# A recurrence in two halves: a state of keys times values instead of the scores between the halves

## The chip, the cores and the metric

The kernel runs on one core of a Trainium2 chip. The metric is device time in microseconds (us) of one execution. TensorE does the matrix products, VectorE, ScalarE and GpSimd the elementwise work, and SyncE issues the transfers of weights and activations.

## What is computed

Two layers of an encoder over 512 positions and 1024 features: a mixer layer with three branches, then cross attention and a feed-forward layer. One of the branches is a gated linear recurrence (HGRN2) with eight heads, in both directions; the change is in it alone. For each head and direction, cut to what matters:

```
f     = lb + (1 - lb) * sigmoid(z)           # decay per position and key feature (128)
log_f = log(max(f, TINY));  key = (1 - lb) * sigmoid(-z)
state = state * f + key^T value              # state is 128 x 64
o     = q . state                            # 64 values per position
o_total = rmsnorm(o_forward + o_backward, g_out) * silu(g)
```

The reference does it in chunks of 16 positions with the state carried over (`_gated_scan`); the backward direction is the same on the flipped sequence.

## The kernel before

It holds no state at all. For every pair of positions it forms a score, the query decayed from a reference point times the key decayed up to it, and then one product of scores with values gives the output of both directions. Per head:

- `take_q`, `take_z` take the projected query and the two gates out of PSUM (ScalarE; two sigmoids per direction).
- `hgrn_decay`, once per direction d: ScalarE's L407, VectorE's two clips L410 and L411, ScalarE's two logarithms L412 and L413, GpSimd's sum L414, the running sum along the sequence on VectorE (`scan`, L417), small sums at 16 reference points, three exponentials on ScalarE (L437, L441, L442), decayed queries `qd` (L444) and inverse-decayed keys `ki` (L445), and eight products L463 into the tile `lt`: four levels i of block sizes (32, 64, 128, 256 positions) for keys (VectorE) and for queries (GpSimd).
- `hgrn_scores`: TensorE's score matmuls. 64 small ones for the diagonal blocks of 128 positions (banks `bd`, `bb`), then the cross scores in three banks `g`, eight matmuls with 1536 columns in all: four of 128 columns within a half of the sequence and four of 256 between the halves. Two masked copies take the diagonal out (L491, L492), ScalarE's L494 and VectorE's four small additions L496 put it into the tile `a`, and three copies L511 on ScalarE put the cross scores there.
- the output block, once per pair of heads: eight matmuls of 512 columns with the values as weights (64 wide, the pair's two heads on opposite halves of the output's partitions).

The heads run as a pipeline: while head i's scores and the projections of head i + 2 are on TensorE, the elementwise engines do the decay of the next head. All other TensorE work in the stretch is projections: each weight arrives from memory as `wraw`, is split into a high part `whi` (ScalarE, L120) and a low part `wlo` (VectorE, L121), and takes three matmuls (L151) per 128 x 128 block, so a projection to 128 columns is 24 matmuls. The order of each engine's instructions is fixed when the kernel is built, by a scheduler that takes TensorE's program order as it is written; every engine runs its own list strictly in that order.

Of the kernel before, what the change touches and what calls it, by code (L numbers as in the profile page):

```python
# [12 lines left out]
AF = mybir.ActivationFunctionType  # L13
ALU = mybir.AluOpType
AX = mybir.AxisListType

P = 128
D = 1024
T = 512
# [56 lines left out]
class _K:  # L76
# [214 lines left out]
    def hgrn(self, l, x, xg, acc, sd):  # L291


        nc = self.nc
        lv = V_N * l
        ar = np.arange(P)
        heads = [dict(n=i) for i in range(8)]
        off = dict(q=O_BQ, f=O_FF, b=O_FB, i=O_BI, g=O_BG)
        proj = lambda o, n: self.projs("w_in", l, np.arange(D), [off[o] + n * P + ar], h)[0]
        vs, st = {}, {}  # L300

        def take_q(hd, b):
            hd["q"] = self.t2()
            nc.scalar.activation(hd["q"], b, AF.Copy)

        def take_z(hd, zs, gs=()):
            for c, b in gs:
                self.gate_put(sd, c, b)
            for d, z in enumerate(zs):
                s, k = self.t2(), self.t2()  # L310
                nc.scalar.activation(s, z, AF.Sigmoid)
                last = nc.scalar.activation(k, z, AF.Sigmoid, scale=-1.0)
                hd[d] = (s, k)
            hd["pin"] = self.pin(last)

        def late():
            st["r"] = self.rstd(acc, 1024)
            st["h"] = self.normed(x, st["r"], lv + V_GMIX)

        def decay(hd):  # L320
            hd["qk"] = self.c8([P, 4, T])
            with self.tc.issue_after(hd["pin"].ins):
                for d in range(2):
                    self.hgrn_decay(l, hd, d)

        def values(n):
            st["vf"] = self.t2()
            nc.scalar.activation(st["vf"], proj("i", n), AF.Copy)

        b0, b1, bq, bv = self.projs("w_in", l, np.arange(D), [off[o] + ar for o in "fbqi"], xg, late, 3)  # L330
        h, r = st["h"], st["r"]
        take_z(heads[0], [self.timed(b, r) for b in (b0, b1)])
        heads[0]["q"] = self.timed(bq, r)
        st["vf"] = self.timed(bv, r)
        decay(heads[0])
        g0, g1, b0, b1 = self.projs("w_in", l, np.arange(D), [O_GB + ar, O_GB + P + ar, off["f"] + P + ar,
                                                             off["b"] + P + ar], h)
        take_z(heads[1], [b0, b1], [(0, g0), (1, g1)])
        take_q(heads[1], proj("q", 1))
        vs[0] = self.vturn(st["vf"])  # L340
        values(1)
        self.hgrn_scores(heads[0])
        decay(heads[1])
        y = self.pairs4(4)
        for i in range(8):
            pr = i // 2
            if i > 0:
                self.hgrn_scores(heads[i])
            if i % 2 == 0:
                if 0 < i < 6:  # L350
                    values(pr + 1)
            gs = [(i + 2, self.gate_proj(l, O_GB, i + 2, h))] if i < 6 else []
            if i % 2 == 1:
                g = proj("g", pr)
                sg = self.t2()
                last = nc.scalar.activation(sg, g, AF.Sigmoid)
                if i == 7:
                    self.pin(last)
                nc.vector.tensor_tensor(sg, g, sg, op=ALU.mult)
            if i < 6:  # L360
                take_z(heads[i + 2], [proj("f", i + 2), proj("b", i + 2)], gs)
            elif i == 6:
                pre = self.mla_pre(l, h)
                for nm in ("ckv0", "ckv1", "key"):
                    pre[nm]()
            else:
                for nm in ("cq0", "nckv", "cq1", "rope"):
                    pre[nm]()
            if i % 2 == 1:

                ob = self.bank()
                for j in range(4):
                    for e in range(2):
                        hf = slice(64 * e, 64 * e + 64)
                        self.mm(ob[hf], vs[pr][:, j, hf], heads[i - 1 + e]["a"][:, j * T:(j + 1) * T], j == 0, j == 3)
                osb, sq = self.t2(), self.t2()
                nc.scalar.activation(osb, ob, AF.Copy)
                nc.scalar.activation(sq, osb, AF.Square)
            if i < 6:
                take_q(heads[i + 2], proj("q", i + 2))  # L380
                if i % 2 == 0:
                    vs[pr + 1] = self.vturn(st["vf"])
            elif i == 7:
                pre["cq2"]()
            if i % 2 == 1:
                ob = self.bank()
                self.mm(ob, self.cst[:, C_BONE:C_BONE + P], sq, True, True)
            if i < 6:
                decay(heads[i + 2])
            elif i == 7:  # L390
                pre["ncq"]()
            if i % 2 == 1:
                r = self.t2()
                self.rsqrt(r, ob, 64)
                nc.vector.scalar_tensor_tensor(r, osb, self.col(lv + V_GOUT), r, op0=ALU.mult, op1=ALU.mult)
                nc.vector.tensor_tensor(r, r, sg, op=ALU.mult)
                self.split(y[pr][0], y[pr][1], r)
        return y, h

    def hgrn_decay(self, l, hd, d):  # L400

        nc = self.nc
        tt = nc.vector.tensor_tensor
        c = d * 8 + hd["n"]
# [4 lines left out]
        g = self.t2()  # L409
# [37 lines left out]
        for i in range(4):  # L447
            n, nb = 1 << i, 8 >> i
            for w, (src, ex) in enumerate(((qd, eq), (ki, ek))):
                half = (1 - d) if w == 0 else d  # L450
                eng = nc.gpsimd if w == 0 else nc.vector
                sv = src.rearrange("p (b s n i) -> p b s n i", s=2, n=n, i=32)[:, :, half]
                ev = ex[:, 16 * i:16 * i + 16].rearrange("p (b s n) -> p b s n", s=2, n=n)[:, :, half]
                ov = lt[:, i, w].rearrange("p (b n i) -> p b n i", n=n, i=32)
                if n == 1:
                    sv, ev, ov = sv[:, :, 0], ev[:, :, 0], ov[:, :, 0]
                    ev = ev.unsqueeze(2).to_broadcast([P, nb, 32])
                elif nb == 1:
                    sv, ev, ov = sv[:, 0], ev[:, 0], ov[:, 0]
                    ev = ev.unsqueeze(2).to_broadcast([P, n, 32])  # L460
                else:
                    ev = ev.unsqueeze(3).to_broadcast([P, nb, n, 32])
                eng.tensor_tensor(ov, sv, ev, op=ALU.mult)  # L463
        hd["lt", d] = lt

    def hgrn_scores(self, hd):

        nc = self.nc
# [6 lines left out]
        for j in range(4):  # L475
# [9 lines left out]
            for g in range(4):  # L485
# [1 line left out]
                lt = lf if g < 2 else lr  # L487
                cs = slice(64, 128) if g < 2 else slice(0, 64)
                one(bd[q4[g], j, cs], lt[:, 1, 1, ks], lt[:, 1, 0, 64 * j:64 * j + 64])
        a = self.c8([P, 4 * T])  # L490
        nc.vector.copy_predicated(self.zz, self.msk[:, 0].unsqueeze(1).to_broadcast([P, 4, P]), bd)  # L491
        nc.vector.copy_predicated(self.zb, self.msk[:, 1, 0:32].unsqueeze(1).to_broadcast([P, 4, 32]), bb)  # L492
        dg = bass.AP(a.tensor, a.offset, [list(a.ap[0]), [640, 4], [1, P]])
        nc.scalar.activation(dg, self.zz, AF.Copy)  # L494
        for g in range(4):
            tt(dg[q4[g], :, q4[g]], self.zz[q4[g], :, q4[g]], self.zb[q4[g]], op=ALU.add)  # L496
        h0, h1 = slice(0, P), slice(P, 2 * P)
        for i in range(3):
            g = self.bank()
            if i == 0:  # L500
                one(g[:, 0:128], lf[:, 2, 1, h0], lf[:, 2, 0, h0])
                one(g[:, 128:384], lf[:, 3, 1, h0], lf[:, 3, 0])
                one(g[:, 384:512], lr[:, 2, 1, h0], lr[:, 2, 0, h0])
            elif i == 1:
                one(g[:, 0:256], lf[:, 3, 1, h1], lf[:, 3, 0])
                one(g[:, 256:512], lr[:, 3, 1, h0], lr[:, 3, 0])
            else:
                one(g[:, 0:128], lf[:, 2, 1, h1], lf[:, 2, 0, h1])
                one(g[:, 128:384], lr[:, 3, 1, h1], lr[:, 3, 0])
                one(g[:, 384:512], lr[:, 2, 1, h1], lr[:, 2, 0, h1])  # L510
            nc.scalar.activation(a[:, i * 640 + 128:(i + 1) * 640], g, AF.Copy)  # L511
        hd["a"] = a

    def gates(self, l, gate, h):

# [17 lines left out]
    def gate_put(self, sd, c, b):  # L533
        sg = self.t2()
        last = self.nc.scalar.activation(sg, b, AF.Sigmoid)
        self.nc.sync.dma_start(sd[:, c], sg)
        return last

    def branch(self, l, sd, wname, rows, y, merged, first):

# [639 lines left out]
```

## Time and profile before

| | |
|---|---|
| median of 3 runs | 2372.4 us (2371.82 to 2373.35) |
| the profiled execution | 2371.25 us, its span 2369.5 us |
| busy share | TensorE 99%, VectorE 62%, ScalarE 50%, GpSimd 7% |
| granted TensorE clock, mean | 0.999 of full speed |

The rows are one execution, seen instruction by instruction. A row of a timeline gives start, length, engine, line, operation, output and inputs, and in brackets the idle time before it with what ended it. The length of a row reaches a little into the next one's, so costs are better taken from start to start.

### The profile page before, as it was taken

What the parts mean: (1) busy time and instruction counts of PE and PEld (TensorE: products, weight loads), DVE (VectorE), ACT (ScalarE), POOL (GpSimd) and SP (SyncE); (2) the same over time, 40 slices, a digit from 0 to 9 for tenths busy, and PEclk for the clock granted to TensorE, in tenths of its full rate; (3) what the DMA queues carried; (4) which work ended last, traced back from release to release, by engine and by line L of the source; (5) the groups of instructions that cost most, each with busy time, mean ns of one, the idle gap of its engine ahead of it and who ended that gap; (6) DMA issues with size and microseconds to landing.
All of it is one profiled execution on the core that took longest, in us unless ns stands there. A gap on an engine that the chain in (4) does not pass through costs nothing.

```text
span 2369.5 us, 34666 instructions
## 1 busy us (share of the span) xinstructions
PE 2336.9 (99%) x12934; PEld 1901.6 (80%) x12934; DVE 1469.8 (62%) x2753; ACT 1187.3 (50%) x2162; POOL 167.8 (7%) x165
## 2 busy tenths in 40 slices
PE   9999999999999999999999999999999999999998
PEld 7877778777888888888887777777788888888886
DVE  8876756566756555355577866666657575553553
ACT  7766566556545433233367656655555454332332
POOL 1332300000000000000013322000000000000000
PEclk9999999999999999999999999999999999999999
DMA  4223233234553233333432223322345523333332
GB/s 163 86 86 94 84 96 103 80 98 134 196 148 89 80 94 98 98 96 96 130 106 87 84 69 102 98 85 91 95 140 178 147 76 94 94 98 98 96 96 76
DMA packets 133513, 246.26 MB, mean 104 GB/s; under 512 B 14816, under 2 KB 17120, under 8 KB 132960
## 3 DMA queue, kind: packets, MB, share of 16 engines
q1 hardware_dynamic: 133344, 244.05, 33.5%
q8 instruction: 101, 1.65, 0.3%
q14 instruction: 68, 0.56, 0.1%
HBM read 227.22 MB, written 16.78 MB: 103 GB/s over the span
## 4 chain that ended last, share of the span: by engine, by line
PE 85%; DVE 6%; issue 4%; POOL 2%; ACT 2%; DMA 1%; POOLq 0%; DVEq 0%; SPq 0%; ACTq 0%
PE ps L151 83%; POOL c L463 1%; PE ps L658 1%; DVE c L463 1%; DVE t L417 1%; POOL t L414 1%; DVE wlo L121 1%; DVE c L444 1%; PE ps L790 1%; DVE c L445 0%; ACT whi L120 0%; PE ps L939 0%; DMA t<-in_bias_dram 0%; DMA wraw<-in_w_dram 0%; PE ps L286 0%
## 5 line engine op out<-in xcount | busy, mean ns | idle before, releaser
L151 PE MATMUL ps<-c,whi 128*128 128x512 f32 (+1 forms) x5696 | 1733.9, 387 | 5.9 <-ACT whi L120 5.9
L151 PEld LDWEIGHTS ps<-c,whi 128*128 128x128 f32 x5696 | 1058.3, 188 | 236.8 <-issue 16.9
L151 PE MATMUL ps<-c,wlo 128*128 128x512 f32 (+1 forms) x2848 | 1096.9, 385 | 6.5 <-DVE wlo L121 6.5
L120 ACT ACTIVATE whi<-wraw 128x512 fp32r<-128x512 f32 x764 | 475.1, 629 | 817.3 <-PE ps L151 606.4
L121 DVE TENSOR_TENSOR wlo<-wraw,whi 128x512 fp32r<-128x512 f32 x764 | 526.5, 697 | 545.7 <-ACT whi L120 535.9
L151 PEld LDWEIGHTS ps<-c,wlo 128*128 128x128 f32 x2848 | 535.7, 188 | 116.2 <-DVE wlo L121 9.1
L151 PE MATMUL ps<-c,t 128*64 128x512 f32 (+6 forms) x960 | 167.5, 418 | 4.5 <-DVE smw L767 2.3
L151 PEld LDWEIGHTS ps<-c,t 128*64 128x64 f32 (+2 forms) x960 | 99.7, 167 | 55.3 <-issue 31.6
L988 DVE TENSOR_TENSOR t<-ps,t 128x512 f32<-128x512 f32 x112 | 76.3, 689 | 103.3 <-PE ps L151 103.3
L463 POOL TENSOR_TENSOR c<-c,smx 128x256 f32<-128x256 f32 x128 | 122.8, 988 | 111.0 <-DVE c L444 82.8
L414 POOL TENSOR_TENSOR t<-t,t 128x512 f32<-128x512 f32 x32 | 44.1, 1379 | 1184.4 <-ACT t L413 1169.0
L970 DVE TENSOR_TENSOR c<-ps,c 128x512 f32<-128x512 f32 x64 | 44.2, 690 | 70.1 <-PE ps L151 70.1
L463 DVE TENSOR_TENSOR c<-c,smx 128x256 f32<-128x256 f32 x128 | 81.6, 695 | 0.2
L151 PEld LDWEIGHTS ps<-c 128*32 128x32 f32 (+1 forms) x2304 | 61.2, 120 | 12.2 <-PE ps L151 5.3
L151 PE MATMUL ps<-c 128*32 128x32 f32 (+3 forms) x2304 | 69.3, 218 | 0.2
L180 ACT ACTIVATE c<-ps 128x512 fp32r<-128x512 f32 (+2 forms) x78 | 42.7, 547 | 39.9 <-PE ps L151 38.9
L181 DVE TENSOR_TENSOR c<-ps,c 128x512 fp32r<-128x512 f32 (+2 forms) x78 | 49.3, 632 | 20.8 <-ACT c L180 20.4
L441 ACT ACTIVATE t<-t 128x512 f32<-128x512 f32 x32 | 20.1, 629 | 79.7 <-DVE t L440 79.7
L417 DVE TENSOR_TENSOR_SCAN t<-cst,t 128x512 f32<-128x512 f32 x32 | 39.0, 1220 | 23.7 <-POOL t L414 23.7
L181 DVE TENSOR_TENSOR c<-t,c 128x512 fp32r<-128x512 f32 (+1 forms) x84 | 51.6, 634 | 3.3 <-ACT c L180 3.3
L180 ACT ACTIVATE c<-t 128x512 fp32r<-128x512 f32 (+1 forms) x84 | 48.0, 581 | 8.6 <-DVE t L982 3.5
L645 ACT ACTIVATE t<-ps,sm 128x512 f32<-128x512 f32 x64 | 43.5, 687 | 12.6 <-DVE sm L643 12.5
(144 smaller groups left out, 1788.2 us busy)
## 6 DMA issues: line engine op xcount, KB each, us to landing
wraw<-in_w_dram SPq DMA_DIRECT2D x764, 256.0 KB, 2.6
gate<-t SPq DMA_DIRECT2D x32, 256.0 KB, 2.3
t<-gate SPq DMA_DIRECT2D x32, 256.0 KB, 3.9
c<-in_xT_dram SPq DMA_DIRECT2D x16, 256.0 KB, 5.5
gate_b<-t SPq DMA_DIRECT2D x16, 256.0 KB, 3.4
t<-gate_b SPq DMA_DIRECT2D x16, 256.0 KB, 3.8
t<-in_bias_dram SPq DMA_DIRECT2D x16, 192.0 KB, 3.6
c<-in_memT_dram SPq DMA_DIRECT2D x3, 1024.0 KB, 8.2
```

The costliest lines, as they stand in the source:

```text
L120: self.nc.scalar.activation(hi, raw, AF.Copy)
L121: self.nc.vector.tensor_tensor(lo, raw, hi.bitcast(F32), op=ALU.subtract)
L151: self.nc.tensor.matmul(o, a, b, start=start, stop=stop)
L180: nc.scalar.activation(hi, src, AF.Copy)
L181: nc.vector.tensor_tensor(lo, src, hi.bitcast(F32), op=ALU.subtract)
L414: nc.gpsimd.tensor_tensor(f, f, g, op=ALU.add)
L417: scan = lambda o, m, x: nc.vector.tensor_tensor_scan(o, m, x, 0.0, op0=ALU.mult, op1=ALU.add)
L444: tt(qd, hd["q"], f, op=ALU.mult)
L463: eng.tensor_tensor(ov, sv, ev, op=ALU.mult)
L645: nc.scalar.activation(p, s, AF.Exp, bias=nm, accum_out=sm)
L970: nc.vector.tensor_tensor(x[c], b, xold[c], op=ALU.add)
L988: self.nc.vector.tensor_tensor(t, b, r, op=ALU.mult)
```

## The change

Within each half of the sequence the scores stay as they are. Between the halves there are no scores any more. Per head and direction the inverse-decayed keys of the half that comes first (`lt[:, 3, 1]`) are transposed on TensorE (bank `kb`), copied by ScalarE to `kt` (L532), multiplied with that half's values in the new `hgrn_states` into a state of 128 x 64, which VectorE copies to `st` (L565), and the output block multiplies the states with the decayed queries of the other half. GpSimd writes those queries into an own tile `q3` instead of into `lt`. The four cross matmuls of 128 columns go into one bank `bn` with one copy L530, and `a` becomes smaller. In lines of the changed kernel: L428 is the former L407, L431 and L432 the clips, L433 and L434 the logarithms, L438 the scan, L458, L462 and L463 the exponentials, L465 and L466 `qd` and `ki`, L485 the products, L526 and L529 the diagonal, L555 the gates' sigmoid (L535 before).

TensorE's program has the state matmuls behind the gate projection of head i for heads 0 to 5, behind `ckv0` of the attention branch for head 6, behind the projection `g` for head 7.

```diff
         def decay(hd):
             hd["qk"] = self.c8([P, 4, T])
+            hd["q3"] = self.t2(shape=(P, 2, 2 * P))
...
             gs = [(i + 2, self.gate_proj(l, O_GB, i + 2, h))] if i < 6 else []
+            states = lambda: self.hgrn_states(heads[i], vs[pr][:, :, 64 * (i % 2):64 * (i % 2) + 64])
+            if i < 6:
+                states()
             if i % 2 == 1:
                 g = proj("g", pr)
+                if i == 7:
+                    states()
...
-                for nm in ("ckv0", "ckv1", "key"):
-                    pre[nm]()
+                pre["ckv0"]()
+                states()
+                pre["ckv1"]()
+                pre["key"]()
...
-                for j in range(4):
-                    for e in range(2):
-                        hf = slice(64 * e, 64 * e + 64)
-                        self.mm(ob[hf], vs[pr][:, j, hf], heads[i - 1 + e]["a"][:, j * T:(j + 1) * T], j == 0, j == 3)
+                for hv in range(2):
+                    for n in range(3):
+                        for e in range(2):
+                            hf, hd = slice(64 * e, 64 * e + 64), heads[i - 1 + e]
+                            if n < 2:
+                                w, m = vs[pr][:, 2 * hv + n, hf], hd["a"][:, 2 * hv + n]
+                            else:
+                                w, m = hd["st"][:, 1 - hv], hd["q3"][:, 1 - hv]
+                            self.mm(ob[hf, 2 * P * hv:2 * P * hv + 2 * P], w, m, n == 0, n == 2)
...
+        bn = self.bank([P, 4, P])
+        for j, lt in enumerate((lf, lr, lf, lr)):
+            js = slice(P * (j // 2), P * (j // 2) + P)
+            one(bn[:, j], lt[:, 2, 1, js], lt[:, 2, 0, js])
+
+        kb = self.bank([P, 4, P])
+        for j in range(4):
+            nc.tensor.transpose(kb[:, j], (lf, lr)[j // 2][:, 3, 1, P * (j % 2):P * (j % 2) + P], self.ident)
...
-        for i in range(3):
-            g = self.bank()
...
-            nc.scalar.activation(a[:, i * 640 + 128:(i + 1) * 640], g, AF.Copy)
-        hd["a"] = a
+        nc.scalar.activation(at(P, P), v4(bn), AF.Copy)
+        kt = hd["kt"] = self.t2(shape=(P, 4, P))
+        nc.scalar.activation(kt, kb, AF.Copy)
...
+    def hgrn_states(self, hd, v):
+
+        sb = self.bank([P, 2, 64])
+        for d in range(2):
+            for j in range(2):
+                self.mm(sb[:, d], hd["kt"][:, 2 * d + j], v[:, 2 * d + j], j == 0, j == 1)
+        self.nc.vector.tensor_copy(hd["st"], sb)
```

The change also moves instructions on the elementwise engines. ScalarE of the kernel before, around head 5 of layer 0: `t_434` and `t_438` (first and second direction) are gates of head 6 in their decay, `c_444` is the score tile `a` of head 5.

```order
L412 ACTIVATE t_434_2465<-t_434_2465 128x512
L413 ACTIVATE t_419_2408<-t_419_2408 128x512
L412 ACTIVATE t_438_2496<-t_438_2496 128x512
L413 ACTIVATE t_421_2412<-t_421_2412 128x512
L441 ACTIVATE t_419_2408<-t_435_2471 128x512
L437 ACTIVATE smx_2473<-smx_2473 128x128
L442 ACTIVATE t_435_2471<-t_435_2471 128x512
L120 ACTIVATE whi_2672<-wraw_2633 128x512
L441 ACTIVATE t_421_2412<-t_439_2502 128x512
```

And of the changed kernel at the same place, where `t_447` and `t_451` are these gates, `c_393` is head 5's `a` and `t_459` its `kt`:

```order
L433 ACTIVATE t_447_2506<-t_447_2506 128x512
L434 ACTIVATE t_431_2448<-t_431_2448 128x512
L526 ACTIVATE c_393_2201<-zz_102 128x2x2x128
L530 ACTIVATE c_393_2201<-ps_2633 128x2x256
L462 ACTIVATE t_431_2448<-t_448_2512 128x512
L458 ACTIVATE smx_2514<-smx_2514 128x128
L463 ACTIVATE t_448_2512<-t_448_2512 128x512
L120 ACTIVATE whi_2717<-wraw_2672 128x512
L433 ACTIVATE t_451_2537<-t_451_2537 128x512
L120 ACTIVATE whi_2739<-wraw_2697 128x512
L434 ACTIVATE t_433_2452<-t_433_2452 128x512
L532 ACTIVATE t_459_2651<-ps_2638 128x512
```

The second direction's logarithms, which ran ahead of the first direction's exponentials, now follow them, and the copy to `kt` stands behind both.

VectorE before, at the same head:

```order
L410 TENSOR_SCALAR t_434_2465<-t_419_2408 128x512
L411 TENSOR_SCALAR t_419_2408<-t_419_2408 128x512
L492 COPY_PREDICATED zz_102<-msk_159,ps_2527 128x128
L491 COPY_PREDICATED zz_102<-msk_159,ps_2526 128x512
L417 SCALAR_TENSOR_TENSOR t_435_2471<-cst_86,t_419_2408 128x512
L410 TENSOR_SCALAR t_438_2496<-t_421_2412 128x512
L430 COPY smx_2473<-t_435_2471 128x16
L411 TENSOR_SCALAR t_421_2412<-t_421_2412 128x512
```

VectorE of the changed kernel, further down in the same decay, from the last small sums of the first direction to the scan of the second:

```order
L457 TENSOR_TENSOR smx_2514<-smx_2514 128x64
L529 TENSOR_TENSOR c_393_2201<-zz_102 32x2x2x32 x2
L465 TENSOR_TENSOR c_445_2503<-t_442_2494,t_431_2448 128x512
L466 SCALAR_TENSOR_TENSOR c_445_2503<-t_432_2449,small_64,t_448_2512 128x512
L529 TENSOR_TENSOR c_393_2201<-zz_102 32x2x2x32
L485 TENSOR_TENSOR c_450_2527<-c_445_2503,smx_2514 128x256 x4
L431 TENSOR_SCALAR t_451_2537<-t_433_2452 128x512
L121 TENSOR_TENSOR wlo_2718<-wraw_2672,whi_2717 128x512
L432 TENSOR_SCALAR t_433_2452<-t_433_2452 128x512
L121 TENSOR_TENSOR wlo_2740<-wraw_2697,whi_2739 128x512
L438 SCALAR_TENSOR_TENSOR t_452_2543<-cst_86,t_433_2452 128x512
```

The clips of the second direction, which stood right behind the first scan, now stand behind the four products of the first direction; the small additions on the diagonal, which stood at the end, are spread ahead of them.

ScalarE in the first heads of layer 0, before: the second decay of head 0 (`t_73`, `t_83`), then the sigmoids of two gates (L535) and of head 1.

```order
L441 ACTIVATE t_73_353<-t_83_401 128x512
L437 ACTIVATE smx_403<-smx_403 128x128
L442 ACTIVATE t_83_401<-t_83_401 128x512
L535 ACT_TABLE_LOAD
L535 ACTIVATE t_114_573<-ps_425 128x512
L535 ACTIVATE t_115_576<-ps_426 128x512
L311 ACTIVATE t_116_579<-ps_427 128x512
```

The same place after:

```order
L555 ACT_TABLE_LOAD
L555 ACTIVATE t_115_574<-ps_426 128x512
L458 ACT_TABLE_LOAD
L458 ACTIVATE smx_404<-smx_404 128x128
L462 ACTIVATE t_73_353<-t_84_402 128x512
L555 ACT_TABLE_LOAD
L555 ACTIVATE t_116_577<-ps_427 128x512
L463 ACT_TABLE_LOAD
L463 ACTIVATE t_84_402<-t_84_402 128x512
L311 ACT_TABLE_LOAD
L311 ACTIVATE t_117_580<-ps_428 128x512
```

Sigmoids and exponentials, which stood in two groups, now alternate, with a table load at each turn; a sixth load (L232) follows in both kernels.

## Rows read from the trace of the kernel before

**Rows 1.** The page: busy time by engine, and granted clock in 40 slices.
```profile
PE 2336.9 (99%) x12934; PEld 1901.6 (80%) x12934; DVE 1469.8 (62%) x2753; ACT 1187.3 (50%) x2162; POOL 167.8 (7%) x165
...
PEclk9999999999999999999999999999999999999999
```

**Rows 2.** Timeline of TensorE (PE), layer 0, around the scores of head 5.
```profile
230.46 0.60 PE L286 MATMUL ps<-cst,t 128*128 128x128 f32 x4
230.98 4.30 PE L151 MATMUL ps<-c 128*32 128x32 f32 x144
235.04 0.70 PE L151 MATMUL ps<-c,whi 128*128 128x512 f32 x2
...
240.61 0.61 PE L151 MATMUL ps<-c,whi 128*128 128x512 f32 x2
```

**Rows 3.** Timeline of TensorE, the output block of heads 0 and 1.
```profile
118.28 3.65 PE L151 MATMUL ps<-c,t 128*64 128x512 f32 x16
```

**Rows 4.** Timeline of VectorE (DVE), decay of head 6 beside head 5's scores.
```profile
234.68 1.23 DVE L417 TENSOR_TENSOR_SCAN t<-cst,t 128x512 f32<-128x512 f32 x1 [1.26 <-POOL t L414]
235.82 0.40 DVE L410 TENSOR_SCALAR t<-t 128x512 f32<-128x512 f32 x1
...
237.97 1.63 DVE L444 TENSOR_TENSOR c<-t,t 128x512 f32<-128x512 f32 x1
...
245.53 0.69 DVE L121 TENSOR_TENSOR wlo<-wraw,whi 128x512 fp32r<-128x512 f32 x1
246.13 0.69 DVE L444 TENSOR_TENSOR c<-t,t 128x512 f32<-128x512 f32 x1
246.73 0.75 DVE L445 SCALAR_TENSOR_TENSOR c<-t,small,t 128x512 f32<-128x512 f32 x1
...
248.43 2.69 DVE L463 TENSOR_TENSOR c<-c,smx 128x256 f32<-128x256 f32 x4
251.04 1.17 DVE L496 TENSOR_TENSOR c<-zz 32x128 f32<-32x128 f32 x4
```

**Rows 5.** Timeline of ScalarE (ACT), the same stretch.
```profile
245.01 0.63 ACT L441 ACTIVATE t<-t 128x512 f32<-128x512 f32 x1 [5.73 <-DVE t L440]
...
247.43 1.55 ACT L511 ACTIVATE c<-ps 128x512 f32<-128x512 f32 x3
```

**Rows 6.** Timelines of TensorE and VectorE: heads 1 and 4, scores and next scan.
```profile
90.84 4.31 PE L151 MATMUL ps<-c 128*32 128x32 f32 x144
97.44 1.23 DVE L417 TENSOR_TENSOR_SCAN t<-cst,t 128x512 f32<-128x512 f32 x1 [1.25 <-POOL t L414]
...
196.51 4.30 PE L151 MATMUL ps<-c 128*32 128x32 f32 x144
199.26 1.23 DVE L417 TENSOR_TENSOR_SCAN t<-cst,t 128x512 f32<-128x512 f32 x1 [1.11 <-POOL t L414]
```

**Rows 7.** Timeline of ScalarE, layer 0, a table load behind head 1's sigmoids.
```profile
60.31 1.28 ACT L232 ACT_TABLE_LOAD   x1
```

**Rows 8.** Timeline of VectorE, layer 0, last products ahead of head 1's scores.
```profile
87.17 2.26 DVE L463 TENSOR_TENSOR c<-c,smx 128x256 f32<-128x256 f32 x4
```

**Rows 9.** The page, costliest groups: matmuls with wlo; last, idle before.
```profile
L151 PE MATMUL ps<-c,wlo 128*128 128x512 f32 (+1 forms) x2848 | 1096.9, 385 | 6.5 <-DVE wlo L121 6.5
```

**Rows 10.** Windows: length, busy PE, PEld, DVE, ACT, POOL, clock, DMA.
```profile
2358.00:2362.80 4.80, 1.12 (x2) 0.30 (x2) 1.69 (x3) 1.83 (x3) 0.00 (x0) 1.00 0.01 4
2362.90:2369.40 6.50, 0.00 (x0) 0.00 (x0) 3.60 (x6) 0.00 (x0) 0.00 (x0) 0.50 0.81 314
```

**Rows 11.** Timeline of TensorE at the program's start.
```profile
5.88 1.22 PE L151 MATMUL ps<-c,whi 128*128 128x512 f32 x2 [5.88 <-ACT whi L120]
...
8.62 1.06 PE L151 MATMUL ps<-c,whi 128*128 128x512 f32 x2
...
9.90 1.06 PE L151 MATMUL ps<-c,whi 128*128 128x512 f32 x2
...
11.13 0.63 PE L151 MATMUL ps<-c,whi 128*128 128x512 f32 x2
```

More of the change, by code (lines that the diff above doesn't have):

```diff
@@ L318, in late, with pair_a @@
             st["h"] = self.normed(x, st["r"], lv + V_GMIX)
+        def pair_a(i):
+            a, st = self.c8([P, 2, 4, 2 * P]), self.t2(shape=(P, 2, 2, 64))
+            for e in range(2):
+                heads[i + e]["a"], heads[i + e]["st"] = a[:, e], st[:, e]
         def decay(hd):
             hd["qk"] = self.c8([P, 4, T])
+            hd["q3"] = self.t2(shape=(P, 2, 2 * P))
             with self.tc.issue_after(hd["pin"].ins):
@@ L341, in hgrn @@
         values(1)
+        pair_a(0)
         self.hgrn_scores(heads[0])
@@ L347, in hgrn @@
             if i > 0:
+                if i % 2 == 0:
+                    pair_a(i)
                 self.hgrn_scores(heads[i])
@@ L371, in hgrn @@
                 ob = self.bank()
-                for j in range(4):
-                    for e in range(2):
-                        hf = slice(64 * e, 64 * e + 64)
-                        self.mm(ob[hf], vs[pr][:, j, hf], heads[i - 1 + e]["a"][:, j * T:(j + 1) * T], j == 0, j == 3)
+                for hv in range(2):
+                    for n in range(3):
+                        for e in range(2):
+                            hf, hd = slice(64 * e, 64 * e + 64), heads[i - 1 + e]
[4 more added lines that the diff above has]
+                            self.mm(ob[hf, 2 * P * hv:2 * P * hv + 2 * P], w, m, n == 0, n == 2)
                 osb, sq = self.t2(), self.t2()
@@ L453, in hgrn_decay @@
                 ev = ex[:, 16 * i:16 * i + 16].rearrange("p (b s n) -> p b s n", s=2, n=n)[:, :, half]
-                ov = lt[:, i, w].rearrange("p (b n i) -> p b n i", n=n, i=32)
+                ov = hd["q3"][:, d] if i == 3 and w == 0 else lt[:, i, w]
+                ov = ov.rearrange("p (b n i) -> p b n i", n=n, i=32)
                 if n == 1:
@@ L489, in hgrn_scores @@
                 one(bd[q4[g], j, cs], lt[:, 1, 1, ks], lt[:, 1, 0, 64 * j:64 * j + 64])
-        a = self.c8([P, 4 * T])
+        bn = self.bank([P, 4, P])
[5 more added lines that the diff above has]
+            nc.tensor.transpose(kb[:, j], (lf, lr)[j // 2][:, 3, 1, P * (j % 2):P * (j % 2) + P], self.ident)
+        a = hd["a"]
         nc.vector.copy_predicated(self.zz, self.msk[:, 0].unsqueeze(1).to_broadcast([P, 4, P]), bd)
         nc.vector.copy_predicated(self.zb, self.msk[:, 1, 0:32].unsqueeze(1).to_broadcast([P, 4, 32]), bb)
-        dg = bass.AP(a.tensor, a.offset, [list(a.ap[0]), [640, 4], [1, P]])
-        nc.scalar.activation(dg, self.zz, AF.Copy)
+        at = lambda o, st: bass.AP(a.tensor, a.offset + o, [list(a.ap[0]), [4 * P, 2], [st, 2], [1, P]])
+        v4 = lambda t: t.rearrange("p (b c) q -> p b c q", c=2)
+        nc.scalar.activation(at(0, 3 * P), v4(self.zz), AF.Copy)
         for g in range(4):
-            tt(dg[q4[g], :, q4[g]], self.zz[q4[g], :, q4[g]], self.zb[q4[g]], op=ALU.add)
-        h0, h1 = slice(0, P), slice(P, 2 * P)
-        for i in range(3):
-            g = self.bank()
[L500 to L510, printed above, removed]
-            nc.scalar.activation(a[:, i * 640 + 128:(i + 1) * 640], g, AF.Copy)
-        hd["a"] = a
+            d4 = at(0, 3 * P)[q4[g], :, :, q4[g]]
+            tt(d4, v4(self.zz)[q4[g], :, :, q4[g]], v4(self.zb)[q4[g]], op=ALU.add)
+        nc.scalar.activation(at(P, P), v4(bn), AF.Copy)
+        kt = hd["kt"] = self.t2(shape=(P, 4, P))
+        nc.scalar.activation(kt, kb, AF.Copy)
     def gates(self, l, gate, h):
```

## The prediction

> **What bounds the kernel now.** I read the page first, then timelines of single stretches. The page shows TensorE busy 99% of the span and its clock granted in full in all 40 slices [rows 1]: every microsecond that TensorE saves is won, and every one it stands still is lost, since nothing later takes it up. So two things decide: how much TensorE work the change takes away, and whether TensorE, which runs its instructions strictly in the written order, comes to a matmul whose operand isn't there.
>
> **TensorE's work.** The score block of head 5 in layer 0 takes 235.04 - 230.98 = 4.06 us [rows 2]. A 128-wide fp32 matmul is two records here, each of which takes 0.43 us for 512 columns: the 16 records of an output block, with 64-wide weights, take 3.65 us though its two heads fill opposite halves of the array [rows 3], so that a pair of such records takes 2 x 0.228 = 0.46 from row to row, and I use 0.43 (0.84 ns a column) as the pace without the row's ends. Of 1536 cross columns 512 stay: -1024 x 2 x 0.84 ns = -1.72 us a head. Four 128-column transposes come: four such in the same stretch take 230.98 - 230.46 = 0.52 [rows 2], +0.52. The four state matmuls, 64 columns each, have no row. By columns they are 4 x 2 x 64 x 0.84 ns = 0.43; if the load of 128-wide weights sets the pace, each of the 8 records costs at most what a transpose does, 8 x 0.13 = 1.04. I take 0.88, nearer the transposes, since a record of 64 columns is shorter than the load ahead of it. Together -0.32 a head, x16 = -5.1.
>
> The Trainium skill ("TensorE: Matmul & The Clock Gate", section "LDWEIGHTS (loading the stationary operand)") says that loading takes a time set by the number of weight columns, not of rows; by it a record with 128 weight columns could not be shorter than an estimated 0.107 us. That speaks against the count by columns, by which the whole of this term would be -12.3 instead of -5.1. The transposes' 0.13 a piece is in line with it.
>
> The output block: eight matmuls of 512 columns become twelve of 256, that is 16 records of 0.43 in pairs, 3.44 us, to 24 of 0.215 in pairs, 2.58 us: -0.86 for each of 8 pairs of heads = -6.9. **TensorE's sum: -12.0.**
>
> **The new wait.** This is what I think decides. Before, nothing on TensorE needed a result of the cross scores until the output block, which for heads 0 and 1 comes 27 us behind head 1's scores [rows 3, 6]; the three copies on ScalarE ran at 247.43, 16 us after the first score matmul [rows 5], and cost nothing. Now `hgrn_states` stands on TensorE right behind the gate projection and needs `kt`, a copy on ScalarE. The order shown above has that copy behind both Ln of the next head's second decay; these wait for VectorE's clips; and the clips, which stood ahead of all products before, now stand behind the four products of the first decay.
>
> When does TensorE get there in heads 3 and 5? With D for the first score matmul (230.98): the block shrinks to 4.06 - 1.72 + 0.52 = 2.86, and 24 projection matmuls follow, 240.61 - 235.04 = 5.57 [rows 2]. D + 8.43 = 239.4.
>
> When is `kt` there? The first scan begins at 234.68, 3.7 after D, and its successor at 235.82 [rows 4]. From there to the first product 237.97 lie 2.15, of which two clips (about 0.33 each from start to start), now gone from this place, are 0.65: 237.3. Three of the four small additions on the diagonal, 1.17 us for four [rows 4], now stand in between: 238.2. qd 0.60 and ki 0.66 (0.69 and 0.75, of which 0.09 overlap with the next row [rows 4]): 239.5; the fourth addition: 239.8; four products, 251.04 - 248.43 = 2.61: 242.4; clip, one wlo (0.60 from 245.53 to 246.13) and clip: 243.8. ScalarE's second Ln takes 0.63 like its other passes over 512 columns [rows 5]: 244.4; the `kt` copy, one 512-column copy out of PSUM, 1.55 / 3 = 0.52 and some 0.07 for its end: 245.0. The wait is 245.0 - 239.4 = 5.6 us, in heads 3 and 5 of two layers: **+22.4.** The two ends: 4.5 if the additions run in gaps, 7 if VectorE is held up beside GpSimd, as the 1.63 us of one product may show [rows 4].
>
> Heads 2 and 4 have a value projection as well before their states, 24 matmuls more, so TensorE comes at D + 14.0; the chain of an even head starts 0.95 earlier (first scan 199.26 - 196.51 = 2.75 after D against 3.7 [rows 6]) and ends at D + 13.1: no wait. Head 6 has 24 matmuls (`ckv0`) and that chain: 5.6 - 0.95 = 4.65, twice **+9.3**. Head 0 has its copy ahead of the Ln and head 7 no next decay: none.
>
> Head 1: its next decay begins late, the first scan 97.44 - 90.84 = 6.6 after D [rows 6], 2.9 later than in head 5. So at least 5.6 + 2.9 = 8.5. At most, if ScalarE's four sigmoids (2.1, at the copies' 0.52 each), two table loads of 1.28 [rows 7] and three copies of 0.52 all lie between the decays, 5.6 + 6.3 = 11.9. I take the middle, 10.2, twice: **+20.4**.
>
> **The start of the stage.** Sigmoid and Ln/Exp need different tables on ScalarE. Behind head 0's second Ln the order now has five loads in between sigmoids and exponentials and a sixth at the end, where there were two: 4 x 1.28 = 5.1 in layer 0. In layer 1 the whole count of loads grows by two: 2.6. In both layers head 1's second decay is later by the four products, 2.26 [rows 8], that were already done in the shadow of other work. Head 1's scores need these results; the slack is what lies between the end of the last product, 89.43, and the first score matmul, 90.84: 1.4 [rows 6, 8]. 5.1 + 2.3 - 1.4 = 6.0 and 2.6 + 2.3 - 1.4 = 3.5: **+9.5**, with 0 as its lower end if the sigmoids wait for nothing that TensorE needs.
>
> **Weights.** wlo, the low part of a weight tile, is made by VectorE; all waits of TensorE behind it are 6.5 us now [rows 9]. In the changed order I count one behind a second decay's products at each of heads 2 and 4 in both layers, 4 x 2.26 = 9.0: **+2.5**. The copies and POOL's products cost nothing: as many as before or fewer, and ScalarE stands idle for 5.73 us in that stretch [rows 5].
>
> **The clock.** After the last matmul the granted clock shows 0.50, that is 1.2 GHz; in the 4.8 us ahead of it, in which TensorE worked 1.12, it is still 1.00 [rows 10]. At the start of the program three matmuls take 1.28 us (8.62 to 9.90) [rows 11], where later they take 5.57 / 8 = 0.70 [rows 2], and the slow pace lasts from 5.88 to 11.13: (1 - 0.70/1.28) x 5.25 = 2.4 us lost by one start from rest. The two stops at head 1 surely cost that, the six of 4.7 to 5.6 us may: 2 to 8 starts. I take 5: **+12.0** (ends 0 and 19.2).
>
> The Trainium skill (same page, section "🔬 Part 1: The HAM clock gate (the "warmup" mystery)") calls the lower clock the default that activity lifts, which fits the slow first rows; by it a stop costs more than its length, and a forecast without it would be 12 lower.
>
> **Sum.** -12.0 + 22.4 + 9.3 + 20.4 + 9.5 + 2.5 + 12.0 = +64.1. The profiled execution took 2371.25, 1.15 under the median 2372.4: 2371.25 + 64.1 + 1.15 = 2436.5, rounded 2437.
>
> **Rivals.**
> (a) *Faster: the waits hide.* If `kt` lands within 8.4 us of the first score matmul in every head, -12.0 shows alone: 2372.4 - 12.0 = 2360. That is the point from which it decides; with four heads 3 and 5 waiting over 3 us each it is gone. For it: ScalarE idles and the copy needs nothing but the transposes. Against: engines here take instructions in order, and the Ln ahead of it can't start earlier. 4%.
> (b) *Only heads 1, 3, 5 and 6 wait, each the plain length; no slips at the start, no clock.* -12.0 + 6 x 5.6 + 9.3 + 2.5 = +33.4: 2406; with the clock 2425. For it: the 1.4 us of slack may be more in layer 1. 20%.
> (c) *All stops cost the clock, and head 1 its upper end.* +64.1 + 7.2 + 3.4 = 2447, with VectorE's longer chain (6 x 1.4) 2456, and up to 2470 if the start slips further. 12%.
> (d) *No change,* saving and waits equal: it needs that only two of eight stops remain. 2%.
>
> **How the numbers follow.** The forecast's own case (2422 to 2450) has 62%. The range reaches over (b) and most of (c), 2404 to 2468. I count 0.2%, 4.7 us, as what a measurement tells from no change. Faster: (a), 4%; same: (d), 2%; slower: 94%.
>
> **What the changed profile would show.** TensorE's waits at the state matmuls (L151, weights from `kt`) with ScalarE's copy L532 as releaser: none in heads 0, 2, 4 and 7, about 5 to 6 us in 3, 5 and 6, 8 to 12 in head 1. TensorE's busy time falls by about 12 before clock losses. The clips L431 and L432 of the second decay start after the fourth product L485. Slow triplets of 1.28 follow the longer stops. It would be wrong if ScalarE's copy L532 ran ahead of those Ln on the chip, or if the stops found TensorE late anyway.

## The result and the profile after

The changed kernel takes 2444.1 us (2443.6 to 2444.7, 4 runs) against 2372.6: a ratio of 1.0299, 95% interval 1.0286 to 1.0312, so it is slower by 3.0%. The forecast was 2437, range 2404 to 2468. The profiled execution took 2444.11, its span 2442.3, which is 72.8 more than before.

The page of the changed kernel, where [rows 1] stand for before:

```profile
PE 2349.9 (96%) x13062; PEld 1919.7 (79%) x13062; DVE 1460.5 (60%) x2769; ACT 1190.5 (49%) x2152; POOL 162.4 (7%) x165
...
PE   9798889999999999999998897999999999999998
PEclk9999999999999999999998998999999999999999
```

TensorE's share has fallen from 99 to 96%, and the dips stand in slices 2 to 6 and 22 to 25, in the recurrence stages of the two layers. What TensorE waits for is in the view of the waits, with the sum, the number of times and the longest one:

```profile
PE ps L151 <- ACT t L532: 55.9, 8, 10.4
PE ps L151 <- ACT whi L120: 6.7, 3, 6.1
PE ps L151 <- DVE wlo L121: 4.8, 4, 1.5
PE ps L151 <- DVE c L466: 3.2, 2, 1.7
```

L532 is the copy to `kt`. The eight waits, called stops below since TensorE stands still in them, are 10.4 and 9.8 us in head 1 of the two layers, 6.3 and 6.0 in head 3, 5.9 and 7.2 in head 5, 5.2 and 5.2 in head 6; heads 0, 2, 4 and 7 have none. The second row holds the first weight of the program (about 6 us before too, [rows 11]). Head 5 of layer 0, whose counterparts are [rows 2, 4, 5], on TensorE:

```profile
253.40 2.58 PE L151 MATMUL ps<-c 128*32 128x32 f32 x136
255.81 0.60 PE L520 MATMUL ps<-cst,c 128*128 128x128 f32 x4
256.17 0.70 PE L151 MATMUL ps<-c,whi 128*128 128x512 f32 x2
...
267.75 1.97 PE L151 MATMUL ps<-t,t 128*128 128x64 f32 x8 [5.85 <-ACT t L532]
269.48 1.20 PE L151 MATMUL ps<-c,whi 128*128 128x512 f32 x2
...
270.90 1.05 PE L151 MATMUL ps<-c,whi 128*128 128x512 f32 x2
...
272.18 1.05 PE L151 MATMUL ps<-c,whi 128*128 128x512 f32 x2
...
275.43 0.62 PE L151 MATMUL ps<-c,whi 128*128 128x512 f32 x2
...
276.12 0.62 PE L151 MATMUL ps<-c,whi 128*128 128x512 f32 x2
```

The block of scores and transposes takes 256.17 - 253.40 = 2.77 us. TensorE is through with the projection at 267.75 - 5.85 = 261.9 and stands still. Why, the timelines of ScalarE and VectorE say:

```profile
260.20 0.61 ACT L463 ACTIVATE t<-t 128x512 f32<-128x512 f32 x1
260.72 0.62 ACT L120 ACTIVATE whi<-wraw 128x512 fp32r<-128x512 f32 x1
265.54 0.63 ACT L433 ACTIVATE t<-t 128x512 f32<-128x512 f32 x1 [4.21 <-DVE t L431]
...
266.60 0.61 ACT L434 ACTIVATE t<-t 128x512 f32<-128x512 f32 x1
267.12 0.57 ACT L532 ACTIVATE t<-ps 128x512 f32<-128x512 f32 x1
```

```profile
257.11 1.22 DVE L438 TENSOR_TENSOR_SCAN t<-cst,t 128x512 f32<-128x512 f32 x1 [1.27 <-POOL t L435]
...
262.58 2.59 DVE L485 TENSOR_TENSOR c<-c,smx 128x256 f32<-128x256 f32 x4
265.10 0.41 DVE L431 TENSOR_SCALAR t<-t 128x512 f32<-128x512 f32 x1
```

ScalarE idles 4.21 us and then runs the two logarithms and the copy; the transposes that the copy reads were done at 256.2, eleven microseconds earlier. The logarithm waits for the clip L431, and that one stands behind the four products L485. The windows of the same stretch (length, busy PE, PEld, DVE, ACT, POOL, granted clock, DMA share, GB/s):

```profile
253.00:261.00 8.00, 8.00 (x166) 6.92 (x165) 6.57 (x18) 5.35 (x11) 1.29 (x1) 1.00 0.24 70
261.90:267.70 5.80, 0.00 (x0) 0.00 (x0) 5.20 (x10) 2.15 (x4) 3.07 (x5) 0.72 0.09 14
267.80:274.70 6.90, 6.90 (x20) 5.78 (x21) 5.92 (x14) 1.61 (x4) 3.13 (x4) 0.50 0.18 60
274.80:280.00 5.20, 5.20 (x25) 4.26 (x24) 2.53 (x4) 2.89 (x5) 0.95 (x2) 1.00 0.21 54
```

In the stop the granted clock falls (0.72 on the mean), for the next 6.9 us it is 0.50, that is 1.2 GHz, and there the same three matmuls take 1.28 us (270.90 to 272.18) instead of 0.69 (275.43 to 276.12). In seven of the eight stops the clock falls before the stop ends; in head 6 of layer 1 it still shows 1.00 in the whole stop and falls behind it:

```profile
1515.30:1520.40 5.10, 0.00 (x0) 0.00 (x0) 3.66 (x8) 2.82 (x6) 2.85 (x4) 1.00 0.08 13
1520.50:1527.40 6.90, 6.90 (x20) 5.75 (x21) 6.77 (x17) 4.09 (x9) 2.54 (x1) 0.51 0.42 142
```

### The profile page after: what moved, and what is told of

Its sections match the earlier page's. It is cut to its first block, busy times and chain, and to the rows that moved or that the text cites. A ratio compares the mean times of both kernels' runs of the same rounds, so it can differ in the third digit from the quotient of the medians.

```text
span 2442.3 us, 34888 instructions
## 1 busy us (share of the span) xinstructions
PE 2349.9 (96%) x13062; PEld 1919.7 (79%) x13062; DVE 1460.5 (60%) x2769; ACT 1190.5 (49%) x2152; POOL 162.4 (7%) x165
## 3 DMA queue, kind: packets, MB, share of 16 engines
q8 instruction: 102, 1.67, 0.3%
## 5 line engine op out<-in xcount | busy, mean ns | idle before, releaser
L151 PE MATMUL ps<-c,t 128*64 128x256 f32 (+6 forms) x960 | 155.3, 390 | 5.4 <-DVE smw L795 3.1
L485 POOL TENSOR_TENSOR c<-c,smx 128x256 f32<-128x256 f32 x96 | 96.7, 1032 | 143.8 <-ACT t L463 57.5
L151 PE MATMUL ps<-t,t 128*128 128x64 f32 (+1 forms) x192 | 33.5, 359 | 55.9 <-ACT t L532 55.9
L151 PEld LDWEIGHTS ps<-t,t 128*128 128x128 f32 (+1 forms) x192 | 26.8, 218 | 62.8 <-ACT t L532 60.1
L485 DVE TENSOR_TENSOR c<-c,smx 128x256 f32<-128x256 f32 x128 | 73.8, 635 | 0.4
L438 DVE TENSOR_TENSOR_SCAN t<-cst,t 128x512 f32<-128x512 f32 x32 | 39.1, 1223 | 46.0 <-POOL t L435 46.0
L462 ACT ACTIVATE t<-t 128x512 f32<-128x512 f32 x32 | 20.2, 631 | 78.5 <-DVE t L461 78.5
```

Of the source, the lines that this page charges most:

```text
L151: self.nc.tensor.matmul(o, a, b, start=start, stop=stop)
L438: scan = lambda o, m, x: nc.vector.tensor_tensor_scan(o, m, x, 0.0, op0=ALU.mult, op1=ALU.add)
```

## The experiments

Times of each run are set against the kernel before on the same chip.

**1. State matmuls late.** `states()` is called behind all projections of a head instead of behind the gate projection:

```diff
-            if i < 6:
-                states()
...
             else:
                 for nm in ("cq0", "nckv", "cq1", "rope"):
                     pre[nm]()
+            states()
```

> The state matmuls alone are moved on TensorE: from behind the gate projection to behind all projections of the head, at least 48 matmuls (10.9 us) later; everything else stays as in the changed kernel. Theory (the 55.9 us of waits for the copy to kt, and the slow clock behind them, are due to the place of the state matmuls): the longest wait was 10.4 us, so all eight go, and with them the slow phases: 2444 - 56 - 24 = 2364 us, plus or minus 3, faster than the kernel before by some 8. Rival (the recurrence's own work, its transposes, state matmuls and narrower output products, is dearer than counted, and the wait only lies where TensorE would have stopped anyway for late weights): at most half of it comes back, 2405 or more.

Measured: 2381.7 us, ratio 1.0043 (1.0029 to 1.0056). 62 of the 71.5 us came back, and no wait for the copy is left, so the place was the cause of these waits; but both numbers were missed, since the 17.7 us between 2364 and 2381.7 are neither of the two cases. Its waits show new ones:

```profile
PE ps L151 <- DVE wlo L121: 7.9, 6, 1.9
...
PE ps L151 <- DVE t L560: 4.6, 2, 3.1
PE ps L151 <- POOL c L480: 3.3, 4, 1.4
```

L560 is VectorE's copy of the states. In layer 1 it stands behind four weight tiles, and the output block waits for it:

```profile
1303.27 2.48 DVE L121 TENSOR_TENSOR wlo<-wraw,whi 128x512 fp32r<-128x512 f32 x4
1305.68 0.28 DVE L560 COPY t<-ps 128x128 f32<-128x128 f32 x1
```

```profile
1306.11 0.66 PE L151 MATMUL ps<-t,t 128*64 128x256 f32 x1 [3.06 <-DVE t L560]
```

L480 is the products for the next head's scores. Those waits are short, but behind a stop of 1.39 us within the scores of head 7 of layer 0 the granted clock is 0.58 in 295.3 to 299.3, and it is 0.50 behind a wait of 1.79 us for wlo (227.0 to 230.4) and behind the wait of 3.06 us shown above (1306.1 to 1309.0).

**2. Copy first.** The second decay (the decay's second direction) is written behind the scores, and its ScalarE work queued behind the copy:

```diff
+        def decay1(hd, kt):
+            with self.tc.issue_after(hd["pin"].ins), self.tc.issue_after(kt.ins):
+                self.hgrn_decay(l, hd, 1)
...
                 self.hgrn_scores(heads[i])
+                if i < 7:
+                    decay1(heads[i + 1], heads[i]["kti"])
```

> The state matmuls stay where the change put them; the copy to kt is queued on ScalarE ahead of the next head's second logarithms instead of behind them (the second decay is written behind the scores, and its ScalarE work queued behind the copy). It still stands behind the first direction's exponentials and one weight tile. Theory (the copy is late only because of the logarithms ahead of it): it ends some 5 us earlier, waits of about 0 to 1 us in heads 3, 5 and 6, 3 to 5 in head 1, no or little slow clock in heads 3 to 6: 2370 to 2385 us. Rival (the copy is late because the transposes, or the bank, are late): no change, 2440.

Measured: 2380.0 us, ratio 1.0030 (1.0017 to 1.0044); the waits for the copy are 11.2 us, four of them: 4.0 and 6.1 in head 1, 0.5 in head 6, none in heads 3 and 5. Head 3 of layer 0, ScalarE and then TensorE:

```profile
175.53 0.58 ACT L538 ACTIVATE t<-ps 128x512 f32<-128x512 f32 x1
176.01 0.80 ACT L434 ACTIVATE t<-t,small 128x512 f32<-128x512 f32 x1
179.96 0.63 ACT L439 ACTIVATE t<-t 128x512 f32<-128x512 f32 x1 [3.15 <-DVE t L437]
```

```profile
176.16 1.10 PE L151 MATMUL ps<-t,t 128*128 128x64 f32 x8
```

The copy, L538 here, runs at 175.53; the second direction's first logarithm, L439, still waits for its clip L437 until 179.96, and the state matmuls start at 176.16 without a wait. With the state matmuls in their place and the transposes as they were, bringing the copy forward past the second direction's ScalarE work (and writing the second decay later for it) took 64 us away. The rival falls. Head 1's wait was up to 1 us longer than expected.

**3. Fill the stops.** Matmuls of constants ahead of the state matmuls:

```diff
+        fill = {1: 11, 3: 6, 5: 6, 6: 5}.get(hd["n"], 0)
+        if fill:
+            fb = self.bank()
+            for j in range(fill):
+                self.mm(fb, self.cst[:, C_BONE:C_BONE + P], self.cst[:, 0:T], True, True)
```

> The changed kernel, with matmuls of constants into a bank that nothing reads ahead of the state matmuls: 11 fp32 matmuls of 512 columns (9.5 us) in head 1, 6 (5.2) in heads 3 and 5, 5 (4.3) in head 6, in both layers. They fill the stops without taking what TensorE waits for out of the way. Theory (the slow rows behind the stops, 24 us in all, are TensorE's clock, which falls in a stop): TensorE hardly rests, the slow rows go, the end of each stop stays: 2444 - 20 = 2424 us, 2418 to 2428. Rival (the rows behind a stop are slow because weights or results come late, or the 24 us belong to something else): no gain, 2444 or a little more.

Measured: 2421.5 us, ratio 1.0207 (1.0192 to 1.0221): 22.6 less than the changed kernel, with more work on TensorE. Head 5 now:

```profile
256.38 5.31 PE L151 MATMUL ps<-cst 128*128 128x512 f32 x12
262.46 1.10 PE L151 MATMUL ps<-t,t 128*128 128x64 f32 x8 [0.78 <-ACT t L532]
263.38 0.71 PE L151 MATMUL ps<-c,whi 128*128 128x512 f32 x2
...
264.15 0.62 PE L151 MATMUL ps<-c,whi 128*128 128x512 f32 x2
...
264.85 0.62 PE L151 MATMUL ps<-c,whi 128*128 128x512 f32 x2
```

The state matmuls take 0.92 us to the next row instead of 1.73 (267.75 to 269.48), the three matmuls of a block behind them 0.77 and 0.70 at once, and the granted clock is 1.00 from 256.8 to 268.0. So the slow rows are the clock, and they cost 22.6 us in eight stops, 2.8 each on the mean.

**4. As 1, and the start.** Head 1's sigmoids are queued behind head 0's exponentials:

```diff
-        take_z(heads[1], [b0, b1], [(0, g0), (1, g1)])
+        with self.tc.issue_after(heads[0]["exp"].ins):
+            take_z(heads[1], [b0, b1], [(0, g0), (1, g1)])
```

> As the first of these four (state matmuls late), and at the start of each layer the sigmoids for head 1 are queued behind the exponentials of head 0's second decay, which brings the table loads on ScalarE from 87 back to 81, the number before. Theory (head 1's scores wait in both layers, 3.2 and 2.9 us, because the sigmoids and exponentials alternate and each turn costs a table load of 1.28 us): 3 to 6 us less than the first of the four, about 2359 us. Rival (those scores wait because VectorE now does the second decay behind the first decay's products): the loads don't matter, no gain.

Measured: 2381.1 us, ratio 1.0038 (1.0024 to 1.0051): no different from 1. The first wait at head 1's scores in layer 0 fell from 1.62 to 0.76, the output block's wait for the state copy rose from 1.57 to 3.11. That is the rival's "no gain"; but with the one wait shorter and the other longer this run by itself decides nothing on the loads; run 10 does.

**5. Logarithms together.** Clips and logarithms of both directions in a function of their own, called ahead of both decays, on the changed kernel:

```diff
                 for d in range(2):
+                    self.hgrn_logs(l, hd, d)
+                for d in range(2):
                     self.hgrn_decay(l, hd, d)
```

> The changed kernel, in which the clips and logarithms of both directions are written ahead of the rest of both decays; nothing is added or left out. That puts the second direction's clips back ahead of the first direction's products on VectorE, the second logarithms ahead of the first exponentials on ScalarE, and so the copy to kt behind one weight tile only; the state matmuls stay where they were. Theory (the changed place of the clips made the copy late, and the state matmuls are in a good place otherwise): waits for the copy under 1 us in heads 3, 5 and 6 and 0 to 4 us in head 1, little slow clock, 12 to 14 us of TensorE's work saved: 2358 to 2370 us. Rival (with the copy early, something else that the shorter score block leaves too little time for is late next, VectorE's products for the next head's scores or the state copy, as in the second of the first four): 2375 to 2382, no faster than the kernel before.

Measured: 2400.0 us, ratio 1.0118 (1.0102 to 1.0133). Both numbers were missed. The waits for the copy fell from 55.9 to 24.8 us, not to nearly nothing. Head 3, ScalarE:

```profile
174.25 0.58 ACT L538 ACTIVATE c<-ps 128x512 f32<-128x512 f32 x1
178.32 0.63 ACT L470 ACTIVATE t<-t 128x512 f32<-128x512 f32 x1 [3.49 <-DVE t L469]
...
179.69 0.61 ACT L120 ACTIVATE whi<-wraw 128x512 fp32r<-128x512 f32 x1
180.21 0.58 ACT L540 ACTIVATE t<-ps 128x512 f32<-128x512 f32 x1
```

The copy, L540 here, now stands behind the first direction's exponentials, and TensorE still waits 1.87 us; in head 1 four weight tiles stand ahead of it as well, and it waits 7.0.

**6. As 5, state matmuls one projection later** in heads 1, 3, 5 and 6.

> As the one before, and the state matmuls of heads 1, 3, 5 and 6 stand one more projection (24 matmuls, 5.5 us) later. Theory: what was left of the wait in head 1 goes, 0 to 5 us less than the one before, about 2358 to 2362. Rival (VectorE's copy of the states then stands behind more of its other work, and the output block waits for it, as in the first of the first four): 2 to 6 us more than the one before.

Measured: 2380.5 us, ratio 1.0034 (1.0022 to 1.0047), 19.5 below run 5 and not near 2360: the copy's waits are 2.1 us, but those for weights are 12.3 (wlo, longest 3.0) and 8.8 (whi, the program's first included). Both numbers were missed. The rival named the state copy as the next late thing; it was the weights.

**7. Control: the kernel before, logarithms together.** The same edit as in 5.

> Control: the kernel before, without the change, with its clips and logarithms written in the same new order. Theory (the order of the logarithms matters only because the state matmuls need the copy; the kernel before has no such need): same as before within 2 us. Rival (the new order is better by itself, so that a gain of the two kernels above would not be the recurrence's): 5 us or more below the kernel before.

Measured: 2378.6 us, ratio 1.0026 (1.0016 to 1.0036): slower by 6, which neither case had. The new order itself makes a wlo late at the start of both layers (waits for wlo 8.2 against 6.5 [rows 9], longest 2.6 and 2.5), and behind both the granted clock is 0.50 (47.7 to 50.6 and 1224.9 to 1228.2). Runs 5 and 6 have no such wait in layer 0 and one of 0.5 in layer 1, so this cost cannot simply be taken off them; with an order that has a price of its own in one kernel they are no clean measure of what the recurrence can give.

**8. Copy first, tuned.** Run 2, with head 1's state matmuls behind the projection g, head 6's behind the key projection, head 7's decay left where the change has it, and the sigmoids queued as in 4, in all heads:

```diff
-                take_z(heads[i + 2], [proj("f", i + 2), proj("b", i + 2)], gs)
+                zs = [proj("f", i + 2), proj("b", i + 2)]
+                with self.tc.issue_after(heads[i + 1]["exp"].ins):
+                    take_z(heads[i + 2], zs, gs)
...
-                last = nc.scalar.activation(sg, g, AF.Sigmoid)
+                with self.tc.issue_after(heads[min(i + 1, 7)]["exp"].ins):
+                    last = nc.scalar.activation(sg, g, AF.Sigmoid)
```

> The change with four orders set: the copy to kt ahead of the next head's second logarithms in heads 0 to 5 (as in the second run), the state matmuls of head 1 behind the projection g and of head 6 behind the key projection, each head's sigmoids behind the exponentials of the head before (table loads 77, against 87 in the changed kernel and 81 before). Theory (what the recurrence lost is the eight waits, the slow clock behind them and the loads at the start; its own saving on TensorE is 14 us): waits for the copy under 3 us in all, 2359 to 2366 us, faster than before by 7 to 13. Rival (the elementwise engines have no room: each order that frees TensorE here makes weights, products or state copies late there, as the third to sixth runs began to show): 2372 to 2382.

Measured: 2363.2 us, ratio 0.9960 (0.9948 to 0.9973): 9.5 faster than the kernel before and 81 faster than the change as it was made. Its waits:

```profile
PE ps L151 <- ACT whi L120: 5.9, 1, 5.9
...
PE ps L151 <- ACT t L542: 2.0, 2, 1.7
```

L542 is the copy here; what is left of its waits is 2.0 us, 1.7 of them in head 7 of layer 0. The first row is the program's first weight.

**9. Control: the kernel before, sigmoids queued** as in 8.

> Control: the kernel before, with each head's sigmoids queued behind the exponentials of the head before (table loads 77 against 81), nothing else. Theory (the loads matter only where TensorE waits for ScalarE, and in the kernel before it waits for it nowhere in this stage): the same as before within 2 us. Rival (the order of the sigmoids is a gain by itself): 4 us or more below, and that much of the run ahead of this is not the recurrence's.

Measured: 2373.1 us, ratio 1.0005 (0.9996 to 1.0014), no change. So the order of the sigmoids alone gives the kernel before nothing. Run 8's other order that the kernel before could have, the second decay behind the scores, was not tried on it: of the 6.5 us that it waits for wlo [rows 9] nothing is left in run 8, and whether the recurrence or that order took them away no run shows. How much of the 9.5 is the recurrence's stays open.

**10. As 8, without the sigmoids** of heads 2 and later.

> As the eighth run, with only the sigmoids of head 1 held behind head 0's exponentials and those of the later heads left to the scheduler (table loads 89 against 77): around head 1's second decay sigmoids and exponentials alternate again. Theory (a table load costs only where a result that TensorE needs stands behind it, which is so at heads 1 and 2 of both layers): 3 to 10 us more than the eighth run, 2366 to 2373, with waits of TensorE at the scores or the state matmuls of heads 1 and 2. Rival (the loads hide in ScalarE's idle time): 2363, no difference.

Measured: 2370.3 us, ratio 0.9989 (0.9980 to 0.9998), 7.2 above run 8 as the theory had it. Head 1's second decay in layer 0, ScalarE:

```profile
89.43 1.28 ACT L311 ACT_TABLE_LOAD   x1
90.73 0.60 ACT L311 ACTIVATE t<-ps 128x512 f32<-128x512 f32 x1
91.34 1.28 ACT L470 ACT_TABLE_LOAD   x1
92.64 0.63 ACT L470 ACTIVATE t<-t 128x512 f32<-128x512 f32 x1
```

L470 is the exponential that head 1's scores need. Two loads and a sigmoid, 3.2 us (89.43 to 92.64), stand ahead of it; TensorE waits 3.4 us there. So loads, with the sigmoids that they serve, cost where such a result stands behind them, and four of them fewer gave nothing in run 9.

## Why the prediction was right, and where its sums were off

The mechanism was the one that happened: the same eight places, the same chain of clip, logarithm and copy, the same four heads without a wait. By its terms:

- **The new wait**, +52.1 forecast, 55.9 measured. Head 5's chain ends 267.75 - 253.40 = 14.3 us behind the first score matmul (14.0 forecast), TensorE is there at 8.5 (8.4). Of the four in heads 3 and 5 only head 5 of layer 1, 7.2, lies above the upper end of 7; why, no run shows. Runs 1 and 2 show the place and the copy to be the cause.
- **The clock**, +12.0 by 5 starts of 2.4, the term most mis-sized: all eight stops, from 5.2 us up, brought the clock down, as rival (c) has it. Run 3 measures 22.6. The step that failed is "the six of 4.7 to 5.6 us may". The row of [rows 10] that left it open, 4.8 us with the clock at 1.00, is followed there by one at 0.50, and head 6 of layer 1 shows the same: 1.00 in the stop, 0.51 in the 6.9 us behind it. A clock that holds within a stop does not say that the rows behind it run at it.
- **The start**, +9.5 forecast. Head 1's scores wait 1.67, 0.47 and 0.42 us in layer 0 and 1.50 in layer 1; from their first matmul to the projection behind, head 1's score blocks take 5.95 and 5.72 us, 3.2 and 2.9 longer than the 2.77 of a block without a wait, 6.1 in all (0.42 of it in layer 1 is a wait for whi). How much of it is loads and how much products, this does not split; run 4, with the six loads gone, took some 0.9 off the first wait in layer 0.
- **TensorE's work**, -12.0 forecast. Score blocks fell from 4.06 to 2.77 (256.17 - 253.40), state matmuls without a stop cost 0.83 (233.73 to 234.56 in head 4) and output blocks fell from 3.58 (118.28 to 121.86) to 2.75 (133.06 to 135.81): 16 x (-1.29 + 0.83) + 8 x (-0.83) = -14.0. The 0.83 agrees with the term of 0.88 and not with 0.43 by columns. The rule of the Trainium skill ("TensorE: Matmul & The Clock Gate", section "LDWEIGHTS (loading the stationary operand)") agrees within 3%: 0.83 / 8 = 0.104 us a record, by the rule an estimated 0.107.
- **Weights**, +2.5 forecast, 4.8 - 6.5 = -1.7 measured. The count held: the four waits stand at heads 2 and 4 of both layers. The step that failed is their length, taken as that of the four products, 2.26 us each: they last 1.43, 1.55, 0.94 and 0.84. Why they are shorter stays open.

The measured terms add up to 55.9 + 22.6 + 6.1 - 14.0 - 1.7 = +68.9 of 72.8; of the rest the waits for whi (5.9 before, 6.7 now) and for the tile `smw`, behind the recurrence (2.3 and 3.1), hold some 1.2 that is not counted above, and the remainder stays open. That the forecast, 2437, came within 7 us of 2444.1 is in part luck: the clock and the new wait were together 14.4 too low, and TensorE's work, the start and the weights together 9.6 too high. Rival (a) fell in the sum to the order of ScalarE. With that order alone turned round (run 2) the kernel is still 7 us slower than before, and with four orders set (run 8) it is 9.5 faster, where the sum of TensorE's terms says 14. Of run 1's 17.7 us over its expectation the new waits and the slow clock behind them are seen in its rows, but they were not taken away one at a time, so their shares stay open.

## What to carry to other kernels

An edit that lets TensorE read a result that nobody waited for before turns that result's place in another engine's list into a price: look up what stands ahead of it in that list, and what that in turn waits for, before counting saved columns. In a kernel whose TensorE is 99% busy a stop costs more than its length where the clock falls with it: here stops of 5.2 to 10.4 us cost 2.8 us more on the mean. Moving one copy ahead of two logarithms was worth 64 us here, and a gain (9.5 us, of 14 of saved work) became visible only with three more orders set. A control of the kernel before with the same reorder belongs to each tuned version: one reorder cost 6 us by itself, another nothing, and one is missing here.

## What the runs showed of the hardware that was not expected

Eight stops of 5.2 to 10.4 us cost 22.6 us of clock, 2.8 each on the mean, and the cost does not go with the length: behind the longest, 10.43 us in head 1 of layer 0, the granted clock is 0.50 in 3.8 us (113.8 to 117.6), behind the 5.19 us of head 6 of layer 1 it is 0.51 in 6.9.

In the first run a stop of 1.39 us, within a block of 32-column score matmuls in head 7 of layer 0, was followed by a granted clock of 0.58 over 4.0 us; a stop of the same 1.39 us at the same place of layer 1 (1472.2 to 1473.6) left it at 1.00:

```profile
295.30:299.30 4.00, 3.93 (x112) 3.76 (x113) 3.92 (x7) 0.23 (x1) 1.26 (x3) 0.58 0.13 33
1473.60:1477.60 4.00, 3.74 (x126) 3.35 (x127) 3.94 (x7) 0.75 (x2) 1.78 (x3) 1.00 0.02 7
```

In the kernel before, a stop of 2.25 us among full matmuls had no slow rows behind it (1.00 in 219.9 to 223.9), and in the changed kernel waits of 1.67, 0.47 and 0.42 within the same kind of block left the clock at 1.00 (92 to 97.6). So neither the length of a short stop nor the matmuls around it tell whether the clock falls behind it. What does, no run here settles.
